# Constant matmuls in front, a fused softmax and merge sums on VectorE, later gate transposes, and the sixth down tile in token halves, in an fp32 encoder block

## The chip, the core and the metric

The kernel runs on one core of one Trainium2 chip. The metric is the device time of one execution in microseconds (us). The kernel before took 915.12 us, the median of 3 runs (915.03 to 915.34). All lines named L... are lines of the kernel before.

## What is computed

One block of a hybrid encoder on 512 tokens of width 1024, all in float32. A combined projection of the normalised input feeds three mixers (a bidirectional mLSTM, a 2-D neighbourhood attention, a cross-attention into 256 memory tokens). Their outputs are merged by sigmoid gates, projected and added to the input; a convolutional gated FFN of width 2816 and a last RMSNorm follow.

```python
h = rms_norm(x, mix_norm_g)
ml_q, ml_k, ml_v, ml_o, ml_gates, na_qkv, xa_q, merge_pre = split(h @ w_in)
y_ml = mlstm_branch(...)              # conv + silu on q, k; two scans over the tokens
y_na = neighbourhood_attention(...)   # softmax over an 8 x 16 window, with a bias
y_xa = memory_cross_attention(...)
merged = sum over the branches of sigmoid(gate) * (y @ w_br)
x = x + merged @ w_out
x = x + (gelu(dwconv3(a)) * u) @ w_down    # a, u = split(rms_norm(x) @ w_up)
return rms_norm(x, final_norm_g)
```

## The kernel before

**Every fp32 product is three matmuls.** Weights and activations are split into a high and a low part in a shorter format. `mm3` (L198) then adds high x high (L199), high x low (L200) and low x high (L201) into one PSUM bank. Activations lie with channels on the partitions and the 512 tokens along the free axis, so one tile of 128 output channels over 1024 input channels is 8 x 3 matmuls of 128x512. Weights come from HBM in blocks of up to 512 KB, three blocks ahead (`emit_raw`, L140, on SyncE's queue SP). One block ahead they are split, the high part by ScalarE (L181) and the low part by VectorE (L182). Activations are split in the same way by `split_act` (L205, L206).

**The order.** The source is written in the order in which TensorE shall work, and a scheduler of the language then orders each engine's own queue, by priority and by what its model takes to be ready. Each engine works its queue in order, so an instruction that waits holds everything behind it on that engine.

1. *Front* (L224 to L322). SP issues the first tile of x, then all the small vectors (`vec`, 720 bytes in each partition), then the first weight block in three pieces, then more of x. ScalarE loads its function table at its first instruction. `x_part` scales and splits a tile of x and squares it, GpSimd adds the squares (L304). TensorE runs 8 steps over the input channels, in each 4 tiles of the mLSTM's query (12 matmuls). The sums of squares over the partitions (`rstd_cols`, L261) and the row of 1/rms spread over all partitions (`rstd_row`, L273) stand inside the last two of these steps.
2. *mLSTM keys, token-major values, gates.* The 4 key tiles, each with a convolution and silu (`conv`, `silu2`), then blocks with tokens on the partitions.
3. *Projections with generators beside them.* `step(n)` (L803) advances a Python generator (`ml_all`, `xa_all`, `na_all`) by n pieces on average, and each piece issues some instructions of a mixer. Calls of `step` after every projection so weave the mixers between the projections' matmuls. `ml_prep` (L431) is the front of the mLSTM: it turns the gates (PE transposes L464), scans them (four scans on VectorE, L470 to L480), copies the result (ScalarE, L481), and turns it back (PE transposes L492).
4. *Merge* (L874 to L909). For each of three branches: four times two gate tiles (L887, evicted by L889 and L890), then two tiles of the branch's output projection. The product with the gate is on VectorE (L905, L907), and the sum over the branches on GpSimd (L908). In the second of the three branches the neighbourhood attention runs beside it: one piece is `scores` of one index (L649), `values` of the index two before and `transposes` of the index one before. The softmax in `scores` is an addition of the bias (L661), a maximum (L663), two exponentials with sums (L666, ScalarE), a reciprocal (L667) and two multiplications (L669).
5. *Output projection, FFN in two halves* of 11 inner tiles (HF = 11). In the second half, six down tiles are computed with channels on the partitions over all 512 tokens. In `last_tiles` (L950) the last two tiles are computed so for the first 256 tokens only, and with tokens on the partitions for the other 256 (two tiles t = 2, 3), so that their norm is a sum along the free axis.
6. *End.* The first 256 tokens are normalised through `cols_a`, `row_a`, `scale_a` and stored as `outa` in two stores of 512 KB. These stand inside and behind tile t = 2, scaled partly on GpSimd. The other 256 tokens are stored as `outb` in four stores of 256 KB; the last two of them end the program.

Of the kernel before, what the change touches and what calls it, by code (L numbers as in the profile page):

```python
# [11 lines left out]
F32 = mybir.dt.float32  # L12
# [15 lines left out]
NU = 15  # L28
RM, RB = 0.75, 1.4
# [71 lines left out]
def hybrid_block(ctx, tc, xT, memT, wflat, vecs, gbias, nabias, outa, outb):  # L101
# [38 lines left out]
    def emit_raw(i):  # L140
        key, n = BLOCKS[i]
        _, off, _ = BINDEX[key]
        r = wp.tile([P, BW], F32, tag="raw", name=nm("wr"), bufs=3)
        src = wflat[off:off + P * n].rearrange("(p n) -> p n", p=P)
        if i == 0:
            for a, b in ((0, P), (P, n // 2), (n // 2, n)):
                SY.dma_start(r[:, a:b], src[:, a:b])
        else:
            SY.dma_start(r[:, :n], src)
        raws[i] = r  # L150

# [15 lines left out]
    def emit_split(i):  # L167
        key, n = BLOCKS[i]
        r = raws.pop(i)
        c, hs = halves(i)  # L170
        split[i] = []
        for a, b in hs:
            m = (b - a) * c
            if key[0] == "dnl":
                h, l = lastw(4 * key[1] + a, m)
            else:
                h = wp.tile([P, HWD], F32R, tag="hi", name=nm("wh"), bufs=4)
                l = wp.tile([P, HWD], F32R, tag="lo", name=nm("wl"), bufs=4)
            for u, v in ((0, P), (P, m)) if i == 0 and a == 0 else ((0, m),):
                src = r[:, a * c + u:a * c + v]  # L180
                A.activation(h[:, u:v], src, AF.Copy)  # L181
                V.tensor_tensor(l[:, u:v], src, h[:, u:v].bitcast(F32), op=ALU.subtract)  # L182
# [40 lines left out]

    load_x(0)  # L224
    SY.dma_start(vec, vecs)
# [71 lines left out]
    def x_part(k):  # L297
        split_act(XH[k], XL[k], xk[k], vcol("mix_g", k))
        if k == 0:
            A.activation(acc, xk[k], AF.Square)  # L300
# [4 lines left out]
        load_x(k + 4)  # L305
# [3 lines left out]
    for k in range(KT):  # L309
# [5 lines left out]
        if k == KT - 2:  # L315
            rc = rstd_cols(acc, S, "x")
        wh, wl = ws[k % 2]
        for f in range(4):
            fs = slice(f * P, (f + 1) * P)
            mm3(ps_q[f], wh[:, fs], wl[:, fs], XH[k], XL[k], k == 0, k == KT - 1)  # L320
            if k == KT - 1 and f == 0:
                rb = rstd_row(rc, S, "x")  # L322
# [22 lines left out]
    def proj(key, XHs, XLs, n=S):  # L345
        ws = weights(key)
        ps = mmps()
        for k in range(KT):
            mm3(ps[:, :n], ws[k][0], ws[k][1], XHs[k], XLs[k], k == 0, k == KT - 1)
        return ps  # L350

# [4 lines left out]
    for f in range(4):  # L356
        ps = proj(("mlk", f), XH, XL)
# [73 lines left out]
    def ml_prep():  # L431
# [40 lines left out]
        on = scr()  # L472
# [4 lines left out]
        cu = scr()  # L477
# [6 lines left out]
        rd = dp.tile([2, 4, S], F32, name="rd")  # L484
        V.tensor_tensor(rr[:36], cu[:36], mr[:36], op=ALU.subtract)
# [22 lines left out]
        yield  # L508
# [110 lines left out]
    def na_all(nq, nk, yh, yl):  # L619
# [29 lines left out]
        def scores(i, ops, bt):  # L649
# [11 lines left out]
            V.tensor_tensor(sm, ps, bt, op=ALU.add)  # L661
            smv = sm.rearrange("p (a b) -> p a b", a=2)
            V.tensor_reduce(mx, smv, axis=AX.X, op=ALU.max, negate=True)  # L663
# [4 lines left out]
            for j in range(2):  # L668
                V.tensor_scalar(smv[:, j, :], smv[:, j, :], su[:, j:j + 1], None, op0=ALU.mult)  # L669
# [204 lines left out]
    for br in range(3):  # L874
# [8 lines left out]
        for fp in range(4):  # L883
            tg = []
            for i in range(2):
                f = 2 * fp + i
                ps = proj(("g", br, f), XH, XL)  # L887
# [4 lines left out]
                step(RATE[br])  # L892
# [5 lines left out]
            for i in range(2):  # L898
# [7 lines left out]
                else:  # L906
                    V.scalar_tensor_tensor(tg[i], tg[i], 1.0, ps, op0=ALU.add, op1=ALU.mult)  # L907
                    G.tensor_tensor(mgv(f), mgv(f), tg[i], op=ALU.add)  # L908
# [36 lines left out]
    def power(v):  # L945
        col = tiny(v.shape[-1])
        half["p"] = G.tensor_tensor(col, v, nhalf[:, :v.shape[-1]], op=ALU.pow)
        return col

    def last_tiles(U, UL_):  # L950
# [3 lines left out]
        for f in range(LF, KT):  # L954
            ps = mmps()[:, :Hf]
            fs = slice((f - LF) * P, (f - LF + 1) * P)
            for k in range(HF):
                mm3(ps, ws[k][0][:, fs], ws[k][1][:, fs], U[k][:, :Hf], UL_[k][:, :Hf], k == 0, k == HF - 1)
            xf = x2[f][:, :Hf]
# [3 lines left out]
            V.tensor_tensor(acc3[:, :Hf], acc3[:, :Hf], sq, op=ALU.add)  # L963
            A.activation(xf, xf, AF.Copy, scale=vcol("fin_g", f))

# [23 lines left out]

        for t in range(2, NT):  # L990
# [16 lines left out]
            for k in range(HF):  # L1007
# [5 lines left out]
                if not last and k == 5:  # L1013
                    cols_a()
                    for i in range(LF):
                        turn(i)
            v0 = sums()
            if not last:
                row_a()
            else:  # L1020
# [6 lines left out]
            else:  # L1027
                A.activation(sq, r, AF.Square, accum_out=ss)
                scale_a(G, 6)
                scale_a(V, 0, 1)  # L1030
# [3 lines left out]
            if not last:  # L1034
                with tc.issue_after(half["p"].ins):
                    scale_a(G, 7)
                scale_a(V, 2, 3)
                store_a(0)
# [9 lines left out]
            if not last:  # L1048
                scale_a(V, 4, 5)
                store_a(4)  # L1050

    for hh in range(2):
# [33 lines left out]
        for f in range(KT if hh == 0 else LF):  # L1086
# [121 lines left out]
```

## Time and profile before

| | |
|---|---|
| median of 3 runs | 915.12 us |
| the profiled execution: its time | 915.78 us |
| the profiled execution: its span, first to last instruction | 914.0 us |
| TensorE (PE) busy | 899.4 us, 98% of the span |
| VectorE (DVE) busy | 581.9 us, 64% |
| ScalarE (ACT) busy | 436.8 us, 48% |
| GpSimd (POOL) busy | 132.2 us, 14% |
| moved by DMA | 96.52 MB, 106 GB/s on average |
| first matmul starts | 5.75 us |
| last matmul of a product starts | 906.84 us |

Rows of a timeline read: start in us, duration in us, engine, line, operation, tile written <- tiles read, shape, count, and in brackets the idle time before with what ended it. Rows of a group read: busy us, mean ns of one | idle us before, and what ended it. PE is the matmul, PEld the weight load that runs beside it. Matmuls are pipelined, and consecutive ones overlap in the rows. Their pace is therefore the distance from one start to the next, and a pause of TensorE can be hidden in a busy share.

### The profile page before, as it was taken

Reading aid. Unit: us, or ns where it says so; the run is one execution under the profiler, and the core shown is the slowest. Engines: PE = TensorE matmul, PEld = TensorE weight load, DVE = VectorE, ACT = ScalarE, POOL = GpSimd, SP = SyncE. Lnnn points to the kernel's source line nnn. Section 1 sums busy time; section 2 is a strip of 40 time slices with the busy share of each in tenths; the row PEclk is TensorE's granted clock in tenths of the full one; section 3 lists DMA queues with packets and bytes.
Section 4 is the critical chain, followed back from the end, with each engine's and each line's share of the span. In section 5 each row is a group of like instructions: output and inputs, shape, how many; then the busy total and the mean of one; then the engine's idle time right before and its main releaser. Section 6 shows DMA issues by size and latency. Waiting matters only on the chain.

```text
span 914.0 us, 12141 instructions
## 1 busy us (share of the span) xinstructions
PE 899.4 (98%) x4456; PEld 752.1 (82%) x4456; DVE 581.9 (64%) x1004; ACT 436.8 (48%) x882; POOL 132.2 (14%) x156
## 2 busy tenths in 40 slices
PE   7999999999999999999999999999999999999997
PEld 5899878988888888788888888888888888888887
DVE  7893666746566668895445547777733477777423
ACT  7464446656545556564333435544422344444432
POOL 5000421102040300111121211111100011111012
PEclk9999999999999999999999999999999999999999
DMA  7233532522242423231223432322233322322412
GB/s 263 96 93 105 175 115 93 161 93 93 70 138 70 134 84 119 91 126 62 92 93 126 137 116 74 112 93 92 87 95 95 114 94 93 93 92 87 132 36 93
DMA packets 32939, 96.52 MB, mean 106 GB/s; under 512 B 4056, under 2 KB 7400, under 8 KB 32880
## 3 DMA queue, kind: packets, MB, share of 16 engines
q1 hardware_dynamic: 31296, 92.31, 31.4%
q0 software_dynamic: 1440, 3.17, 1.4%
q8 instruction: 35, 0.57, 0.3%
q10 hardware_dynamic: 144, 0.26, 0.1%
q14 instruction: 24, 0.20, 0.1%
HBM read 92.57 MB, written 3.16 MB: 105 GB/s over the span
## 4 chain that ended last, share of the span: by engine, by line
PE 95%; DVE 2%; issue 1%; DMA 0%; ACT 0%; POOL 0%; SPq 0%; POOLq 0%; DVEq 0%; ACTq 0%
PE mm L199 28%; PE mm L200 28%; PE mm L201 28%; PE at L552 2%; PE at L199 2%; PE at L200 2%; PE at L201 2%; PE at L688 1%; PE at L675 1%; DMA wr<-wflat 0%; PE at L765 0%; PE at L659 0%; PE at L660 0%; DVE s L907 0%; DVE y L663 0%
## 5 line engine op out<-in xcount | busy, mean ns | idle before, releaser
L199 PE MATMUL mm<-u,wh 128*128 128x512 f32 (+1 forms) x1082 | 425.3, 393 | 5.7 <-ACT wh L181 5.7
L201 PE MATMUL mm<-u,wl 128*128 128x512 f32 (+1 forms) x1082 | 423.1, 391 | 0.0
L200 PE MATMUL mm<-u,wh 128*128 128x512 f32 (+1 forms) x1082 | 422.7, 391 | 0.0
L181 ACT ACTIVATE wh<-wr 128x512 fp32r<-128x512 f32 (+3 forms) x299 | 186.0, 623 | 286.1 <-PE mm L200 244.2
L182 DVE TENSOR_TENSOR wl<-wr,wh 128x512 fp32r<-128x512 f32 (+3 forms) x299 | 232.8, 780 | 126.4 <-ACT wh L181 122.4
L199 PEld LDWEIGHTS mm<-u,wh 128*128 128x128 f32 x1082 | 203.9, 188 | 50.3 <-ACT wh L181 6.2
L201 PEld LDWEIGHTS mm<-u,wl 128*128 128x128 f32 x1082 | 203.7, 188 | 45.7
L200 PEld LDWEIGHTS mm<-u,wh 128*128 128x128 f32 x1082 | 204.0, 189 | 44.2 <-DVE u L206 0.3
L1081 POOL TENSOR_TENSOR s<-s,rb 128x512 f32<-128x512 f32 x22 | 29.1, 1325 | 266.4 <-DVE s L1080 258.3
L908 POOL TENSOR_TENSOR u<-u,s 128x512 f32<-128x512 f32 x16 | 22.4, 1401 | 166.1 <-DVE s L907 108.9
L205 ACT ACTIVATE u<-s 128x512 fp32r<-128x512 f32 x34 | 21.4, 629 | 52.3 <-DVE s L1084 50.6
L889 DVE TENSOR_TENSOR s<-mm,rb_x 128x512 f32<-128x512 f32 x24 | 16.6, 692 | 28.8 <-PE mm L201 28.8
L206 DVE SCALAR_TENSOR_TENSOR u<-s,u 128x512 fp32r<-128x512 f32 x34 | 23.5, 692 | 14.7 <-ACT u L205 14.4
L540 ACT ACTIVATE E<-R,bi 128x128 f32<-128x128 f32 x80 | 27.7, 394 | 4.9 <-POOL R L521 4.6
L334 ACT ACTIVATE s<-pad,vec 128x512 f32<-128x512 f32 x30 | 24.4, 813 | 8.4 <-DVE pad L332 8.4
L335 DVE SCALAR_TENSOR_TENSOR s<-pad,vec,s 128x512 f32<-128x512 f32 x30 | 22.5, 750 | 6.1 <-ACT s L334 6.1
L199 PE MATMUL mm<-wh,u 128*128 128x256 f32 (+1 forms) x80 | 24.5, 306 | 0.0
L200 PE MATMUL mm<-wl,u 128*128 128x256 f32 (+1 forms) x80 | 24.3, 304 | 0.0
L201 PE MATMUL mm<-wh,u 128*128 128x256 f32 (+1 forms) x80 | 24.3, 304 | 0.0
L1091 DVE TENSOR_TENSOR u<-mm,u 128x512 f32<-128x512 f32 x14 | 9.7, 692 | 22.2 <-PE mm L201 22.2
L1080 DVE SCALAR_TENSOR_TENSOR s<-s,s 128x512 f32<-128x512 f32 x22 | 15.2, 692 | 13.4 <-ACT s L1079 13.3
L336 DVE SCALAR_TENSOR_TENSOR s<-pad,vec,s 128x512 f32<-128x512 f32 x30 | 22.5, 750 | 0.7
(250 smaller groups left out, 980.6 us busy)
## 6 DMA issues: line engine op xcount, KB each, us to landing
wr<-wflat SPq DMA_DIRECT2D x141, 512.0 KB, 3.5
s<-xT SPq DMA_DIRECT2D x16, 256.0 KB, 4.3
nab<-nabias SPq DMA_DIRECT2D x16, 256.0 KB, 2.7
wr<-wflat SPq DMA_DIRECT2D x15, 192.0 KB, 2.4
R<-rd SPq DMA_DIRECT2D x8, 256.0 KB, 3.6
u<-nav_d POOLq DMA_DIRECT2D x32, 64.0 KB, 3.0
wr<-wflat SPq DMA_DIRECT2D x2, 544.0 KB, 3.2
s<-memT SPq DMA_DIRECT2D x4, 256.0 KB, 3.7
```

The lines of the kernel that those rows point to most:

```text
L181: A.activation(h[:, u:v], src, AF.Copy)
L182: V.tensor_tensor(l[:, u:v], src, h[:, u:v].bitcast(F32), op=ALU.subtract)
L199: PE.matmul(ps, lh, rh, start=start, stop=False)
L200: PE.matmul(ps, lh, rl, start=False, stop=False)
L201: PE.matmul(ps, ll, rh, start=False, stop=stop)
L206: V.scalar_tensor_tensor(l, src, scale, h.bitcast(F32), op0=ALU.mult, op1=ALU.subtract)
L334: A.activation(t1, pad[:, 0:512], AF.Identity, scale=vcol(w, i), bias=vcol(b, i))
L335: V.scalar_tensor_tensor(t1, pad[:, 1:513], vcol(w, n + i), t1, op0=ALU.mult, op1=ALU.add)
L336: V.scalar_tensor_tensor(t1, pad[:, 2:514], vcol(w, 2 * n + i), t1, op0=ALU.mult, op1=ALU.add)
L540: A.activation(E[:, i, :], src, AF.Exp, bias=bi[:, d, abs(J - s), s, h:h + 1])
L908: G.tensor_tensor(mgv(f), mgv(f), tg[i], op=ALU.add)
L1081: G.tensor_tensor(c, c, rb2, op=ALU.mult)
```

## The change

The edits, in the order of the program; the arithmetic of the block stays the same.

- **Front.** VectorE fills a tile of 128x256 with ones, ScalarE takes one small Tanh of it, and TensorE multiplies it with itself 13 times (128x256 each) into a bank that nobody reads. The first 8 columns of `vec` (the input norm's gains) become a DMA of their own on ScalarE's queue, the rest of `vec` and the gate bias `gb` go to the end of SP's first issues, `gb` no longer on GpSimd's queue. The first and the second weight block are issued in pieces between the tiles of x. The high part of the first 128 weight columns is copied by VectorE instead of ScalarE. The square of tile k of x is issued one step later.
- **Norm of x.** `rstd_cols` and `rstd_row` move from the last two steps of the query into the first key tile (behind its steps 1 and 7), and the first two key tiles use the PSUM banks of the pool `at`.
- **mLSTM gates.** Two scan tiles come from another buffer pool, and one yield of `ml_prep` moves ahead of the subtraction L485, one is dropped at the end, so that the turn back L492 comes one piece later.
- **Softmax.** Addition and maximum are one VectorE instruction per half (tensor_tensor_reduce, x2 per piece), followed by a sign change of the [128, 2] maximum; the two multiplications become one tensor_tensor with a broadcast operand.
- **Merge.** Sums on VectorE instead of GpSimd; half of the `step` of a gate tile is called in the middle of its projection.
- **End.** The sixth tile of the second half (index 5) is computed in two token halves in `last_tiles`. The norm of the first 256 tokens is worked out during its second half, all scaling is on VectorE and both `outa` stores come ahead of t = 2. The column sum for v0 (L1002) moves from behind the tile to behind step 3.

```diff
-        if i == 0:
-            for a, b in ((0, P), (P, n // 2), (n // 2, n)):
-                SY.dma_start(r[:, a:b], src[:, a:b])
-        else:
-            SY.dma_start(r[:, :n], src)
         raws[i] = r
+        if i < 2:
+            cuts = (0, P, n // 2, n) if i == 0 else (0, n // 2, n)
+            return [(r[:, a:b], src[:, a:b]) for a, b in zip(cuts, cuts[1:])]
+        SY.dma_start(r[:, :n], src)
...
-                A.activation(h[:, u:v], src, AF.Copy)
+                if i == 0 and a == u == 0:
+                    V.tensor_copy(h[:, u:v], src)
+                else:
+                    A.activation(h[:, u:v], src, AF.Copy)
...
+    warm = cp.tile([P, 256], F32R, name="warm")
+    V.memset(warm.bitcast(F32), 1.0)
+    A.activation(cp.tile([P, 2], F32, name="first"), warm[:, :2].bitcast(F32), AF.Tanh)
+    pw = atps()
+    for _ in range(WARM):
+        PE.matmul(pw[:, :256], warm[:, :P], warm, start=True, stop=True)
+    A.dma_start(vec[:, :8], vecs[:, :8])
+    w0, w1 = emit_raw(0), emit_raw(1)
+    st["raw"] = 2
     load_x(0)
-    SY.dma_start(vec, vecs)
-    emit_raw(0)
-    for k in range(1, 4):
-        load_x(k)
-    emit_raw(1)
-    st["raw"] = 2
-    G.dma_start(gb, gbias[0:16].partition_broadcast(P))
+    SY.dma_start(*w0[0])
+    SY.dma_start(*w0[1])
+    load_x(1)
+    SY.dma_start(*w0[2])
+    load_x(2)
+    SY.dma_start(*w1[0])
+    load_x(3)
+    SY.dma_start(*w1[1])
+    SY.dma_start(vec[:, 8:], vecs[:, 8:])
+    SY.dma_start(gb, gbias[0:16].partition_broadcast(P))
...
+    def proj(key, XHs, XLs, n=S, bank=None, at={}):
+        ws = weights(key)
+        ps = (bank or mmps)()
+        for k in range(KT):
+            mm3(ps[:, :n], ws[k][0], ws[k][1], XHs[k], XLs[k], k == 0, k == KT - 1)
+            if k in at:
+                at[k]()
+        return ps
...
+    ps_k = [proj(("mlk", 0), XH, XL, bank=atps, at={1: lambda: norm.append(rstd_cols(acc, S, "x")),
+                                                    7: lambda: norm.append(rstd_row(norm[0], S, "x"))})]
+    rc, rb = norm
+    ps_k.append(proj(("mlk", 1), XH, XL, bank=atps))
...
-            V.tensor_tensor(sm, ps, bt, op=ALU.add)
             smv = sm.rearrange("p (a b) -> p a b", a=2)
-            V.tensor_reduce(mx, smv, axis=AX.X, op=ALU.max, negate=True)
+            for j in range(2):
+                js = slice(j * M, (j + 1) * M)
+                V.tensor_tensor_reduce(smv[:, j, :], ps[:, js], bt[:, js], 1.0, 2.0 * NEG, ALU.add, ALU.max,
+                                       accum_out=mx[:, j:j + 1])
+            V.tensor_scalar(mx, mx, -1.0, None, op0=ALU.mult)
...
-            for j in range(2):
-                V.tensor_scalar(smv[:, j, :], smv[:, j, :], su[:, j:j + 1], None, op0=ALU.mult)
+            V.tensor_tensor(smv, smv, su.unsqueeze(2).to_broadcast([P, 2, M]), op=ALU.mult)
...
-                ps = proj(("g", br, f), XH, XL)
+                ps = proj(("g", br, f), XH, XL, at={3: lambda: step(RATE[br] / 2)})
...
-                step(RATE[br])
+                step(RATE[br] / 2)
...
-                    G.tensor_tensor(mgv(f), mgv(f), tg[i], op=ALU.add)
+                    V.tensor_tensor(mgv(f), mgv(f), tg[i], op=ALU.add)
...
+        for f in range(LF - 1, KT):
+            half_tile(f, slice(0, Hf))
...
+        half_tile(LF - 1, slice(Hf, S), {5: cols_a, HF - 1: row_a})
+        for i in (0, 4):
+            scale_a(V, *range(i, i + 4))
+            store_a(i)
...
+                if k == 3:
+                    v0 = sums()
...
-        for f in range(KT if hh == 0 else LF):
+        for f in range(KT if hh == 0 else LF - 1):
```

Here `half_tile(f, cs, at)` is the old loop body of `last_tiles` for the token range `cs`; it calls `at[k]()` behind step k and takes the weights of tile 5 from its own two blocks.

More of the change, by code (lines that the diff above doesn't have):

```diff
@@ L471, in ml_prep @@
         V.tensor_tensor_scan(mr[32:36, ::-1], lr[32:36, ::-1], pl[96:100, ::-1], NEG, op0=ALU.add, op1=ALU.max)
-        on = scr()
+        on = tp.tile([P, 2 * M], F32, tag="nab", name=nm("on"))
         G.memset(on[:36], 1.0)
@@ L476, in ml_prep @@
         G.memset(onv[32:36, :, P - 1:P], 0.0)
-        cu = scr()
+        cu = tp.tile([P, 2 * M], F32, tag="nab", name=nm("cu"))
         G.memset(cu[:36], 0.0)
@@ L1012, in last_tiles @@
                     A.activation(r, pts[1][:, 256:], AF.Copy)
-                if not last and k == 5:
-                    cols_a()
+                if k == 3:
+                    v0 = sums()
+                if not last and k == HF - 3:
                     for i in range(LF):
                         turn(i)
[L1017 to L1020, printed above, removed]
+            if last:
                 for i in range(LF):
@@ L1033, in last_tiles @@
             col = power(v)
[L1034 to L1038, printed above, removed]
             oa, ob = scr(), scr()
```

44 lines of the change are left out of this document (20 added, 24 removed).

## The prediction

> **What bounds the kernel now.** I read the page first, then the waits of TensorE, then the timeline of the stretches which those waits name.
>
> The page:
>
> ```profile
> span 914.0 us, 12141 instructions
> ...
> PE 899.4 (98%) x4456; PEld 752.1 (82%) x4456; DVE 581.9 (64%) x1004; ACT 436.8 (48%) x882; POOL 132.2 (14%) x156
> ```
>
> TensorE is busy for 98% of the span and the change takes no product away from it. So the most that can be won is what TensorE does not spend on products at full pace: 914.0 - 899.4 = 14.6 us of idleness, and whatever part of its busy time runs slowly. Its waits, all of them (us in total, times, longest):
>
> ```profile
> PE mm L199 <- ACT wh L181: 5.7, 1, 5.7
> PE at L688 <- DVE s L680: 1.2, 1, 1.2
> PE at L492 <- ACT s L481: 0.7, 1, 0.7
> PE at L675 <- DVE s L669: 0.6, 1, 0.6
> PE at L688 <- ACT s L678: 0.2, 1, 0.2
> ```
>
> Five waits, 8.4 us: one of 5.7 us before the first matmul, one of 0.7 us at the turned-back gates, and three of together 2.0 us in the neighbourhood attention. The other 6 us lie behind the last product. The front, queue by queue (SP, ScalarE, VectorE, then TensorE around 11 us):
>
> ```profile
> 0.74 0.38 SPq L221 DMA_DIRECT2D s<-xT  x1
> 1.17 0.42 SPq L225 DMA_DIRECT2D vec<-vecs  x1
> 1.64 1.37 SPq L147 DMA_DIRECT2D wr<-wflat  x3
> ```
>
> ```profile
> 0.73 1.28 ACT L300 ACT_TABLE_LOAD   x1 [0.73 <-PEq L1199]
> 3.82 0.63 ACT L300 ACTIVATE acc_x<-s 128x512 f32<-128x512 f32 x1 [1.81 <-DMA s<-xT]
> 4.36 0.70 ACT L205 ACTIVATE u<-s,vec 128x512 fp32r<-128x512 f32 x1
> 5.38 0.31 ACT L181 ACTIVATE wh<-wr 128x128 fp32r<-128x128 f32 x1 [0.32 <-DMA wr<-wflat]
> 6.52 0.52 ACT L181 ACTIVATE wh<-wr 128x384 fp32r<-128x384 f32 x1 [0.83 <-DMA wr<-wflat]
> ```
>
> ```profile
> 5.10 0.75 DVE L206 SCALAR_TENSOR_TENSOR u<-s,vec,u 128x512 fp32r<-128x512 f32 x1 [0.81 <-ACT u L205]
> 5.77 0.29 DVE L182 TENSOR_TENSOR wl<-wr,wh 128x128 fp32r<-128x128 f32 x1
> 7.08 0.56 DVE L182 TENSOR_TENSOR wl<-wr,wh 128x384 fp32r<-128x384 f32 x1 [1.02 <-ACT wh L181]
> ```
>
> ```profile
> 10.68 0.63 PE L201 MATMUL mm<-u,wl 128*128 128x512 f32 x1
> 11.10 0.55 PE L199 MATMUL mm<-u,wh 128*128 128x512 f32 x1
> 11.49 0.39 PE L200 MATMUL mm<-u,wh 128*128 128x512 f32 x1
> 11.72 0.39 PE L201 MATMUL mm<-u,wl 128*128 128x512 f32 x1
> ```
>
> ```profile
> 8.00:10.00 2.00, 2.00 (x6) 1.52 (x6) 1.93 (x3) 2.00 (x4) 0.18 (x1) 1.00 0.91 358
> ```
>
> The first weight piece (the first of the three at 1.64) lands at 5.38; its high part takes 0.31 us, and the first matmul starts at 5.75. From start to start, a 512-wide matmul takes 0.42 us until 11.10 and 0.23 us from 11.49 on. So for 5.35 us (5.75 to 11.10) TensorE ran the 12 matmuls of the first step at about half pace, though the clock column of the windows (the 1.00 ahead of the last two numbers) shows nothing of it. That is busy time in the page, and yet some 2.4 us lost.
>
> **The change, part by part.**
>
> *Front, start.* The first weight piece takes `vec`'s place in SP's queue, 1.17 instead of 1.64, and lands 0.47 us earlier, near 4.9. VectorE copies it in about the 0.29 us of the row of that size: first matmul at 5.2. The other operand needs x (landed at 3.82), the 8 gains and ScalarE's 0.70 us. The gains' DMA is issued near 0.73 if it goes ahead of the table load, and behind table load and Tanh near 2.2. Its landing time is not in the trace; the larger transfer took
>
> ```profile
> vec<-vecs SPq DMA_DIRECT2D x1, 90.0 KB, 2.8
> ```
>
> so the operand is ready near 4.6, or near 5.7. A landing as slow as the first weight piece's (1.64 to 5.38) on top would make 6.6. I take 5.2 for the first matmul, with 6.6 as the end below nothing. The square leaves ScalarE ahead of the scaling, which only helps.
>
> *Front, pace.* 13 matmuls of 256 columns at half of 0.42 us are 2.7 us. VectorE's fill, for which no row stands, is between the 0.29 us of a 128-wide operation here and the 0.75 us of a 512-wide one; with 0.35 us the burst runs from about 1.1 to 3.8, in time in which TensorE waits for DMA. It costs nothing as long as the first operands land later than that. What it gains is the unknown. The trace shows one fact: 5.35 us after TensorE's first matmul the pace doubles. I take it that this counts from the first constant matmul and that a pause of some 1.4 us does not undo it; then the fast pace comes at about 6.5. By then the front waits for data anyway. The second weight piece lands at 6.52 - 0.47 = 6.05, its high part is ready at 6.6 and its low part, with 0.56 us, at 7.15. From there 7 matmuls are left in the step, 7 x 0.23 = 1.6: the second step begins at 8.8 instead of 11.10. With the thirteenth matmul, which still took 0.39, the front gains 2.4 us. If the pace doubles only 5.35 us after 5.2, the gain is 0.55; if data keeps up with the fast pace from 5.2 on, the step ends at 8.0 and the gain is 3.3.
>
> [...]
>
> *Norm of x.* The same matmuls in another place: 0 on TensorE. The query's convolutions start later, and the first two keys hold two banks until VectorE reads them. The bank of the second key must be free when the fourth token tile of the next stage starts, a whole key tile and more behind; 0.
>
> *Gate transposes.* The wait of 0.7 us at L492 is for the four scans and the copy behind them. A whole projection comes between after the change. What is late next, the turned-back rows, is needed two pieces later. 0.7 us gained, between 0 and 0.8.
>
> *Attention.* The wait of 1.2 us is for L680. VectorE right in front of it, and POOL's row of that time:
>
> ```profile
> 372.06 1.41 DVE L182 TENSOR_TENSOR wl<-wr,wh 128x512 fp32r<-128x512 f32 x1
> 373.39 0.67 DVE L663 TENSOR_REDUCE y<-s 128x2 f32<-128x512 f32 x1
> ```
>
> ```profile
> 371.61 1.30 POOL L908 TENSOR_TENSOR u<-u,s 128x512 f32<-128x512 f32 x1 [1.69 <-DVE s L907]
> ```
>
> ```profile
> 353.00:375.00 22.00, 20.74 (x125) 17.62 (x124) 20.14 (x35) 14.93 (x34) 2.59 (x2) 1.00 0.32 99
> ```
>
> VectorE is busy for 20.14 of 22 us here, it is the limit of this stretch. And a weight split takes 1.41 us while GpSimd sums. The groups of VectorE in the attention (busy us, mean ns):
>
> ```profile
> L182 DVE TENSOR_TENSOR wl<-wr,wh 128x512 fp32r<-128x512 f32 x26 | 19.6, 754 | 7.6 <-ACT wh L181 7.6
> L669 DVE TENSOR_SCALAR s<-s,y 128x256 f32<-128x256 f32 x32 | 13.0, 447 | 0.3
> L661 DVE TENSOR_TENSOR s<-at,nab 128x512 f32<-128x512 f32 x16 | 10.9, 680 | 0.0
> L663 DVE TENSOR_REDUCE y<-s 128x2 f32<-128x512 f32 x16 | 10.8, 676 | 0.1
> ```
>
> A sum moved to VectorE costs about the 0.68 us of L661. What it removes is a collision, 1.41 - 0.68 = 0.73 us each: about even in VectorE's time, better where the collision lies ahead of an instruction that TensorE awaits. The fused operation has one relative in the trace, from SBUF alone and as wide:
>
> ```profile
> 907.69 0.43 DVE L1026 CUSTOM_DVE_ANT_0 s<-s 128x256 f32<-128x256 f32 x1
> 908.04 0.08 DVE L1026 DVE_READ_ACCUMULATOR2_ANT y<- 128x1 f32 x1
> ```
>
> Per piece 2 x (0.43 + 0.08) + about 0.2 for the sign = 1.2 us replace 0.68 + 0.68 = 1.36. One broadcast multiplication at 0.68 replaces two of L669 at 0.45 = 0.9. So a piece gives back some 0.4 us, and right in front of L680 at least one collision (the row at 372.06) and one piece lie: about 1.1 us against a wait of 1.2. The half steps in the middle of a gate tile also bring fewer pieces back to back. I take all three waits as gone, 2.0 us, between 0 (the waits only move) and 3.0 (with the restart of the pipeline behind each).
>
> *End.* Tile 5 in halves is the same columns in twice the matmuls: 0 within 0.1. L1002 comes ahead of the last product:
>
> ```profile
> 906.96 0.28 PE L1002 MATMUL at<-ones,acc 128*128 128x1 f32 x2
> ```
>
> 0.2 us lost. The last stores have the queue to themselves, since both `outa` stores are issued earlier. Before, one was 2.3 us ahead of the last:
>
> ```profile
> 907.68 0.52 SPq L988 DMA_DIRECT2D outa<-u  x1
> 909.95 0.33 SPq L1047 DMA_DIRECT2D outb<-s  x1
> ```
>
> ```profile
> outb<-s SPq DMA_DIRECT2D x3, 256.0 KB, 2.9
> outb<-s ACTq DMA_DIRECT2D x1, 256.0 KB, 2.4
> ```
>
> A store takes 2.4 to 2.9 us to land, so between 0 and 0.5 us is gained; I take 0.2. The end gives 0, between -0.5 and +0.5.
>
> **Sum:** 2.4 + 0.7 + 2.0 + 0 = 5.1 us. The profiled execution took 915.78, its span 914.0, so 1.78 us lie around the span and stay. It would take 910.7. It stood 0.66 above the median of the runs; on the median, 915.12 - 5.1 = 910.0.
>
> **Rivals.**
>
> *The burst does not count.* The pace doubles 5.35 us after the first real matmul, or the change doesn't do what it says, since the scheduler sets the burst late, or the gains' DMA. For it: the burst of 2.7 us is shorter than the 5.35 us and a pause follows it. Against it: nothing in the trace says that the pause resets. Front 0.55 instead of 2.4: 911.9. [...]
>
> *The attention's waits stay.* Behind each merge group `step` still asks for 1.6 pieces at once, and the sums now stand in VectorE's own queue between L907 and the softmax. For it: VectorE at 20.14 of 22 us. Against it: the collision right in front of the longest wait. 915.12 - 3.1 = 912.0. With the first rival together: 913.9.
>
> *VectorE becomes the bound, and the kernel slower.* The mechanism is a fused operation that runs slower from PSUM than L1026 from SBUF. A merge group of the attention has 3 x 1.6 = 4.8 pieces, 9.6 fused operations. VectorE has 22 - 20.14 = 1.9 us to spare in the tight group. Four groups must lose 3.1 + 1.8 = 4.9 us before the kernel is slower by 0.2%, 1.2 each, so VectorE's work must grow by 3.1 per group: from 4.8 x 1.36 = 6.5 to 9.6, that is 1.0 us for each fused operation, twice the 0.51 of the row. At 1.3 us it would be 12.5 - 6.5 - 1.9 = 4.1 per group and 915.1 - 3.1 + 16.4 = 928.4. Against it: the row, and L661, which reads PSUM at 0.68 for twice the width.
>
> **How the numbers follow.** The forecast has 0.56, the burst that doesn't count 0.20, the waits that stay 0.15, both 0.05, slower 0.04. About 0.2% (1.8 us) is what a measurement can tell from no change. The first three lie more than that below 915.12, but for 0.01 at their edge: faster 0.90. Both rivals together are the same, with that edge: 0.06. Slower 0.04. The forecast with all its bounds good (3.3 + 0.8 + 3.0 + 0.5 = 7.6) would be 907.5; I cut there at 907.8, and reach above to 912.9, past the two single rivals at 911.9 and 912.0.
>
> **What would show it.** In the profile after: first real matmul near 5.2 and steps of 0.23 us within it from 6.5 on; no wait at L492's successor; the attention's waits for VectorE under 0.5 us in all, and no weight split above 0.8 us there; fused operations at 0.5 us or less; the last two stores landing 2.4 us after their issue. I am wrong in the front if steps of 0.42 us last past 9, in the attention if TensorE's waits for VectorE keep their sum.

## The result and the profile after

The changed kernel takes 910.88 us (median of 6 runs, 909.93 to 911.15) against 915.22 us for the kernel before (6 runs, 915.03 to 915.65): 4.34 us less, ratio 0.995 with the interval 0.9937 to 0.9963. The forecast was 910.0. The profiled execution is the fastest of the six, 909.93 us with a span of 908.1; beside before's profiled 915.78 that is 5.85 us. So one sum has to explain 5.9 us in a pair of traces and 4.3 us in the medians, and that gap was the first thing to find out.

The page of the changed kernel, and its waits of TensorE (us in total, times, longest). From here on, L... in a row is a line of the kernel that the row comes from:

```profile
span 908.1 us, 12239 instructions
...
PE 900.4 (99%) x4502; PEld 755.2 (83%) x4502; DVE 579.5 (64%) x1059; ACT 436.8 (48%) x884; POOL 107.5 (12%) x136
```

```profile
PE at L233 <- DVE warm L229: 1.2, 1, 1.2
PE mm L202 <- ACT u L208: 0.3, 1, 0.3
PE mm L203 <- DVE u L209: 0.3, 1, 0.3
PE at L705 <- DVE s L699: 0.2, 1, 0.2
```

The waits at the gates and in the attention are gone but for 0.2 us; TensorE now begins at 1.2 us, with the constant matmuls. Its front:

```profile
1.19 3.14 PE L233 MATMUL at<-warm 128*128 128x256 f32 x13 [1.19 <-DVE warm L229]
4.66 0.49 PE L202 MATMUL mm<-u,wh 128*128 128x512 f32 x1 [0.34 <-ACT u L208]
...
5.79 0.39 PE L204 MATMUL mm<-u,wl 128*128 128x512 f32 x1
6.02 0.40 PE L202 MATMUL mm<-u,wh 128*128 128x512 f32 x1
```

The first real matmul starts at 4.66 (before: 5.75), and from 5.79 on one follows each 0.23 us. VectorE's groups in the attention (busy us, mean ns):

```profile
L185 DVE TENSOR_TENSOR wl<-wr,wh 128x512 fp32r<-128x512 f32 x28 | 19.2, 687 | 9.9 <-ACT wh L184 8.2 <-PE at L688 1.5
L692 DVE CUSTOM_DVE_ANT_0 s<-at,nab 128x256 f32<-128x256 f32 x32 | 12.5, 418 | 0.0
...
L692 DVE DVE_READ_ACCUMULATOR2_ANT y<- 128x1 f32 x32 | 2.7, 83 | 0.0
```

The fused operation costs 418 + 83 ns, as L1026 of before suggested, and the weight split is back at 687 ns from 754.

To see where the time came from, follow the same VectorE instruction through both programs: an eviction waits for its product, so its start marks TensorE's progress. Four such marks and the last sum, of before and then of after:

```profile
111.75 0.69 DVE L821 TENSOR_TENSOR u<-mm,rb_x 128x512 f32<-128x512 f32 x1 [1.64 <-PE mm L201]
152.63 0.69 DVE L830 TENSOR_TENSOR s<-mm,rb_x 128x512 f32<-128x512 f32 x1 [1.59 <-PE mm L201]
337.88 0.69 DVE L889 TENSOR_TENSOR s<-mm,rb_x 128x512 f32<-128x512 f32 x1 [1.59 <-PE mm L201]
448.15 0.69 DVE L889 TENSOR_TENSOR s<-mm,rb_x 128x512 f32<-128x512 f32 x1 [0.47 <-PE mm L201]
907.25 0.41 DVE L1023 TENSOR_TENSOR s<-mm,s 128x256 f32<-128x256 f32 x1
```

```profile
109.30 0.69 DVE L851 TENSOR_TENSOR u<-mm,rb_x 128x512 f32<-128x512 f32 x1 [1.64 <-PE mm L204]
149.38 0.69 DVE L860 TENSOR_TENSOR s<-mm,rb_x 128x512 f32<-128x512 f32 x1 [1.59 <-PE mm L204]
334.64 0.69 DVE L919 TENSOR_TENSOR s<-mm,rb_x 128x512 f32<-128x512 f32 x1 [1.59 <-PE mm L204]
442.31 0.69 DVE L919 TENSOR_TENSOR s<-mm,rb_x 128x512 f32<-128x512 f32 x1 [1.35 <-PE mm L204]
901.97 0.42 DVE L1063 TENSOR_TENSOR s<-mm,s 128x256 f32<-128x256 f32 x1 [1.92 <-PE mm L204]
```

The first row of each gives the front: 111.75 - 109.30 = 2.45 us gained. From there the distances between marks tell each stage by itself: to the second mark (the gates) 40.88 and 40.08, gained 0.80; from the third to the fourth (the attention) 110.27 and 107.67, gained 2.60; from the fourth to the last sum 459.10 and 459.66, lost 0.56; from it to the span's end (913.96 and 908.13, unrounded) 6.72 and 6.16, gained 0.56. Together 5.85. The same marks in one profiled execution of each later kernel, the distances from unrounded times. Where the pace doubles is an estimate from the distances between the matmuls' starts, good to some 0.2 us:

| kernel | first real matmul | pace doubles | front mark | gates | attention | to the last sum | tail | span |
|---|---|---|---|---|---|---|---|---|
| before | 5.75 | 11.1 to 11.5 | 111.75 | 40.88 | 110.27 | 459.10 | 6.72 | 914.0 |
| after | 4.66 | by 4.7 | 109.30 | 40.07 | 107.67 | 459.65 | 6.16 | 908.1 |
| again | 4.57 | 10.8 | 111.01 | 40.07 | 107.69 | 459.64 | 6.17 | 909.8 |
| warm0 | 4.62 | 8.3 | 109.89 | 40.07 | 107.70 | 459.64 | 6.15 | 908.7 |
| warm16 | 4.77 | by 5.5 | 109.91 | 40.07 | 107.73 | 459.64 | 6.16 | 908.8 |
| warm22 | 6.05 | 7.2 | 109.58 | 40.07 | 107.71 | 459.65 | 6.16 | 908.4 |
| warm28 | 6.58 | by 6.6 | 109.58 | 40.07 | 107.72 | 459.59 | 6.26 | 908.3 |
| u_yield | 4.50 | 9.0 | 110.08 | **40.87** | 107.64 | 460.00 | 6.18 | 910.0 |
| u_merge | 4.48 | 9.3 | 110.53 | 40.07 | **109.41** | 459.55 | 6.44 | 911.3 |
| u_soft | 4.58 | 10.8 | 110.98 | 40.07 | 107.70 | 459.66 | 6.16 | 909.9 |
| u_half | 4.56 | by 4.6 | 109.11 | 40.07 | 107.90 | 459.58 | 6.41 | 908.3 |
| u_end | 4.59 | 10.8 | 111.01 | 40.07 | 107.67 | **459.24** | **7.34** | 910.6 |
| u_vec | **5.00** | 13.1 | 112.81 | 40.07 | 107.69 | 459.65 | 6.25 | 911.7 |
| b_merge | 6.05 | 10.5 | 111.43 | 40.88 | **107.75** | 459.23 | 6.73 | 911.2 |

A stage whose code is the same repeats from execution to execution: the gates to 0.01 us, the attention of the unaltered code between 107.64 and 107.73, the way to the last sum within 0.1 but for u_yield's 460.00, which nothing here explains, the tail within 0.3. The front mark alone wanders widely, from 109.11 to 111.01 in executions with one and the same front. So the edits are read from single traces by stage, and the front from many runs.

### The profile page after: what moved, and what is told of

It reads as the page before. It is cut to its first block, busy times and chain, and to the rows that moved or that the text cites. A ratio compares the mean times of both kernels' runs of the same rounds, so it can differ in the third digit from the quotient of the medians.

```text
span 908.1 us, 12239 instructions
## 1 busy us (share of the span) xinstructions
PE 900.4 (99%) x4502; PEld 755.2 (83%) x4502; DVE 579.5 (64%) x1059; ACT 436.8 (48%) x884; POOL 107.5 (12%) x136
## 4 chain that ended last, share of the span: by engine, by line
PE 96%; DVE 1%; issue 1%; ACT 1%; DMA 1%; SPq 0%; POOLq 0%; POOL 0%; DVEq 0%
PE mm L202 28%; PE mm L203 28%; PE mm L204 28%; PE at L202 2%; PE at L203 2%; PE at L204 2%; PE at L580 2%; PE at L718 1%; PE at L705 1%; DMA s<-xT 1%; PE at L795 0%; PE at L688 0%; PE at L687 0%; PE at L283 0%; PE at L604 0%
## 5 line engine op out<-in xcount | busy, mean ns | idle before, releaser
L202 PE MATMUL mm<-u,wh 128*128 128x512 f32 (+1 forms) x1077 | 420.6, 391 | 0.5 <-ACT u L208 0.3
L203 PE MATMUL mm<-u,wh 128*128 128x512 f32 (+1 forms) x1077 | 417.4, 388 | 0.3 <-DVE u L209 0.3
L204 PE MATMUL mm<-u,wl 128*128 128x512 f32 (+1 forms) x1077 | 417.2, 387 | 0.0
L184 ACT ACTIVATE wh<-wr 128x512 fp32r<-128x512 f32 (+1 forms) x298 | 185.6, 624 | 285.6 <-PE mm L203 241.5
L185 DVE TENSOR_TENSOR wl<-wr,wh 128x512 fp32r<-128x512 f32 (+3 forms) x299 | 228.7, 766 | 121.4 <-ACT wh L184 114.9
L208 ACT ACTIVATE u<-s 128x512 fp32r<-128x512 f32 x34 | 21.4, 630 | 53.1 <-DVE s L1114 50.6
L964 POOL TENSOR_TENSOR acc<-acc,s 128x512 f32<-128x512 f32 x7 | 9.1, 1298 | 223.1 <-ACT s L963 223.1
L367 DVE TENSOR_TENSOR pad<-mm,rb 128x512 f32<-128x512 f32 x22 | 15.1, 692 | 11.6 <-PE mm L204 11.6
```

The costliest lines, as they stand in the source:

```text
L202: PE.matmul(ps, lh, rh, start=start, stop=False)
L203: PE.matmul(ps, lh, rl, start=False, stop=False)
L204: PE.matmul(ps, ll, rh, start=False, stop=stop)
L208: A.activation(h, src, AF.Copy, scale=scale)
```

## The experiments

**The constant matmuls.** The kernel once more, and other counts:

```diff
-WARM = 13
+WARM = 0
```

That is warm0; warm16, warm22 and warm28 have their number there, and again is unaltered.

> The changed kernel once more, unaltered. Its six runs so far lie between 909.93 and 911.15 us, and the one execution with a profile, in which TensorE ran at the fast pace (0.23 us a step) from its first real matmul at 4.66 us on, was the fastest of them. Theory A (the moment at which the pace doubles is not tied to the kernel's own start; where it falls in the front differs from execution to execution): the runs spread again over about 1 us, and this profile may show the doubling at another place, anywhere from 4.7 to about 9 us, with a span longer by half of the time that was spent at the slow pace. Theory B (the pace doubles a fixed time after the first constant matmul; the spread has another place): the fast pace holds from the first real matmul again, and a span longer than 908.1 us differs from the first profile behind the front.

> The changed kernel without the 13 constant matmuls (the count set to 0), all else as it is. Both theories: the first real matmul stays near 4.7 us and its step runs at 0.42 us a matmul. Theory B: the pace doubles 5.35 us behind it as before, at 10.0 us, step 2 begins near 9.8 instead of 8.39, so 1.4 us slower than the first profiled execution: 911.3 us, and the spread of the runs stays as it is. Theory A: it doubles at a moment that differs between executions, 8 to 11.5 us; step 2 begins between 9.5 and 9.8 in all of them, so the runs lie closer together than those with the burst, at 911.3 to 911.8 us. If the burst does nothing at all: the same time as the changed kernel, 910.9 us.

> The changed kernel with 16 constant matmuls instead of 13: they end near 5.0 us instead of 4.33 and close the pause of 0.34 us ahead of the first real matmul, which starts up to 0.4 us later. [...] Theory B: the fast pace from the first real matmul at about 5.0 us, step 2 waits for data as it did: 910.0 to 910.5 us, with a spread that has nothing to do with the front. If it is the pause that sometimes sets the pace back: the spread goes, and the median falls to about 910.0 us.

> The changed kernel with 28 constant matmuls: at 0.21 us each they reach to 7.2 us, less where the pace doubles within them (opened at 4.6 us they would end at 5.9). Theory A: the real matmuls run at the fast pace from their first one in nearly every execution; it starts between 5.9 and 7.2, step 2 begins between 8.6 and 10.0, so the runs lie between 910.1 and 911.6 us, the median near the changed kernel's own, 910.9, or up to 0.5 above. Theory B: the constant matmuls themselves run at 0.11 us each from about 4.6 us on, the first real one starts at 5.9, step 2 at 8.6: 910.1 us in the front's account, in every execution alike.

> The changed kernel with 22 constant matmuls, which reach to 5.9 us at the slow pace. With 13 the pace doubled at 4.7 to 10.9 us in six profiled executions, with 16 at 5, with 28 near 6. [...] If the length alone counts and 22 is too short: the median is that of 13, 910.9 to 911.0 us.

TensorE's front in the second execution of the unaltered kernel:

```profile
1.19 3.15 PE L233 MATMUL at<-warm 128*128 128x256 f32 x13 [1.19 <-DVE warm L229]
4.57 0.80 PE L202 MATMUL mm<-u,wh 128*128 128x512 f32 x1 [0.23 <-ACT u L208]
...
10.22 0.63 PE L202 MATMUL mm<-u,wh 128*128 128x512 f32 x1
10.64 0.46 PE L203 MATMUL mm<-u,wh 128*128 128x512 f32 x1
10.94 0.39 PE L204 MATMUL mm<-u,wl 128*128 128x512 f32 x1
```

The same burst at the same moment, and the slow pace (0.43 us a matmul) until 10.64, 6.07 us behind the first real matmul. This execution is 1.71 us behind the first one at the front mark (111.01 against 109.30), and 1.71 behind at the last sum (903.68 against 901.97). What the rows show to differ between the two is where the pace doubled. In seven profiled executions with this burst it doubled by 4.6 and by 4.7, at 9.0 and 9.3, and three times at 10.8. (By 4.6 is u_half: the rows at 5.69, 5.92 and 6.15 are 0.23 us apart already.) Nor is it a fixed time after the first real matmul: some 6.2 us in this execution, 3.7 in warm0, 5.7 in the kernel before and 4.5 in b_merge, which has the front of the kernel before.

The runs say the same: again 911.03 us (910.00 to 911.62, 5 runs) and warm0 910.99 (910.48 to 911.60, 5 runs). In the median the 13 constant matmuls are worth nothing. A few more are worth something: warm16 910.33 (909.98 to 910.55), warm28 910.16 (909.38 to 910.47), warm22 910.01 (909.59 to 910.25), 5 runs each; against before in the same batches warm22's ratio is 0.9939 (0.9926 to 0.9951), again's 0.995 (0.9937 to 0.9962). The intervals overlap, the runs hardly do: all 15 runs of the three are at or below 910.55; of the 11 with 13 constant matmuls, 8 are above it. The front of warm22:

```profile
1.19 5.07 PE L233 MATMUL at<-warm 128*128 128x256 f32 x22 [1.19 <-DVE warm L229]
6.05 0.63 PE L202 MATMUL mm<-u,wh 128*128 128x512 f32 x1
...
6.90 0.54 PE L204 MATMUL mm<-u,wl 128*128 128x512 f32 x1
7.28 0.39 PE L202 MATMUL mm<-u,wh 128*128 128x512 f32 x1
```

The first real matmul has no idle time in front of it, here and in warm16 and warm28, where the 13 left 0.16 to 0.34 us; the fast pace is there by 5.5 (16), 7.2 (22) and 6.6 (28). Theory B (a fixed time after the first constant matmul) met the times of 16 and 28, and has fallen all the same: the same burst at the same moment was followed by the fast pace by 4.7 and at 10.8. Of theory A the main part stands, a moment that isn't tied to the kernel's start; its forecast that 28 would have a median of 910.9 or more missed. The sentence about the pause came nearest: where the burst reaches the first product, the late cases are gone. Whether it is the pause or the length isn't shown, since 16 are also longer than 13; and the pause's length doesn't sort the seven executions, for the two early ones had 0.34 and 0.24 us and the one with 0.16 doubled at 9.3. Without a pause the pace doubled within some 6.0 us of the start at 1.19 in each of the three traces. Behind a burst of 3.15 us and a pause the fast pace came at once in two executions of seven, and no run here shows what made the difference.

**The first loads.** The gains in their old place:

```diff
-    A.dma_start(vec[:, :8], vecs[:, :8])
     load_x(0)
+    SY.dma_start(vec, vecs)
     SY.dma_start(*w0[0])
...
-    SY.dma_start(vec[:, 8:], vecs[:, 8:])
```

> The changed kernel with the vector of gains loaded whole in its old place, in SP's queue ahead of the first weight piece, instead of 8 of its columns by ScalarE's queue and the rest last. If the early start (first real matmul at 4.6 instead of 5.75 us) comes from the 90 KB that went ahead of the first weight piece: the piece lands about 1 us later and the first real matmul is back at 5.4 to 5.8 us, and later by that much everything behind it, apart from the moment at which the pace doubles. If it comes from VectorE's copy in ScalarE's place, or from the table load that stands earlier: it stays at 4.6 to 4.9 us.

913.21 us (9 runs, 912.31 to 913.55), 2.3 us above the changed kernel. Its longest wait:

```profile
PE mm L202 <- ACT wh L184: 1.5, 1, 1.5
```

The first real matmul, at 5.00, missed the 5.4 to 5.8: the first weight piece lands only 0.45 us later (its copy at 4.51 instead of 4.06), and what the matmul waits for is the scaled x:

```profile
3.70 0.63 ACT L323 ACTIVATE acc_x<-s 128x512 f32<-128x512 f32 x1 [1.48 <-DMA s<-xT]
4.24 0.70 ACT L208 ACTIVATE u<-s,vec 128x512 fp32r<-128x512 f32 x1
```

The gains are there by 3.92, when VectorE first reads them; the scaling (L208) stands behind the square (L323) here, where the changed kernel starts it at 3.89. What the 90 KB delay is the second weight piece, whose high part starts at 6.71 instead of 5.04, and TensorE stands for 1.5 us behind its first matmul. That is a pause too, and the pace doubles at 13.1. The front mark lies at 112.81, 1.8 us behind the changed kernel's late executions (111.0) and even behind the kernel before (111.75) in these traces: what stays gained in the front hangs on the gains being out of the weights' way. The expectation had the wrong piece.

**The gate transposes.**

```diff
         rd = dp.tile([2, 4, S], F32, name="rd")
-        yield
         V.tensor_tensor(rr[:36], cu[:36], mr[:36], op=ALU.subtract)
...
         ml.update(rd=rd, em=em, bi=bi)
+        yield
```

> The changed kernel with the two yields of ml_prep put back where they were (the transposes of the turned-back gates again one projection earlier), all else as it is. My account: the wait of 0.7 us for the copy behind the scans comes back in the profile and from there to the end every eviction is 0.6 to 0.8 us later against those ahead of it; it is seen in the trace, since the moment at which the pace doubles moves the whole execution by up to 1.7 us. The rival account, that the earlier start of everything (2.4 us in the front) or the scans' other buffers took the wait away: no wait comes back, 0.0 us.

The wait is back,

```profile
PE at L520 <- ACT s L509: 0.7, 1, 0.7
```

and the gates' stage takes 40.87 us instead of 40.07: 0.80, all of it this edit's. (911.41 us, 4 runs, 910.89 to 912.01.)

**The attention: three edits undone one by one, and one done alone.**

```diff
-                    V.tensor_tensor(mgv(f), mgv(f), tg[i], op=ALU.add)
+                    G.tensor_tensor(mgv(f), mgv(f), tg[i], op=ALU.add)
```

That is u_merge; b_merge is the kernel before with the same line changed the other way, and nothing else. u_soft:

```diff
-                V.tensor_tensor_reduce(smv[:, j, :], ps[:, js], bt[:, js], 1.0, 2.0 * NEG, ALU.add, ALU.max,
-                                       accum_out=mx[:, j:j + 1])
-            V.tensor_scalar(mx, mx, -1.0, None, op0=ALU.mult)
+            V.tensor_tensor(sm, ps, bt, op=ALU.add)
+            V.tensor_reduce(mx, smv, axis=AX.X, op=ALU.max, negate=True)
...
-            V.tensor_tensor(smv, smv, su.unsqueeze(2).to_broadcast([P, 2, M]), op=ALU.mult)
+            for j in range(2):
+                V.tensor_scalar(smv[:, j, :], smv[:, j, :], su[:, j:j + 1], None, op0=ALU.mult)
```

u_half:

```diff
-                ps = proj(("g", br, f), XH, XL, at={3: lambda: step(RATE[br] / 2)})
+                ps = proj(("g", br, f), XH, XL)
...
-                step(RATE[br] / 2)
+                step(RATE[br])
```

> The changed kernel with the merge sums back on GpSimd, all else as it is. If the collision is what the waits came from: weight splits on VectorE take up to 1.4 us again while GpSimd sums, and at least the wait of 1.2 us in the second merge group comes back: 0.8 to 1.5 us between the first and the last merge group. If the sums are even in VectorE's time and the softmax or the half steps made the room (VectorE at 18.9 of 22 us in the tight stretch, 3.1 us free): the collisions are seen on VectorE, but TensorE's waits stay under 0.4 us and the stretch keeps its length within 0.2 us.

> The changed kernel with the old softmax (sum, reduction, two multiplications) instead of the fused operation and the one multiplication, all else as it is. A piece then costs VectorE 0.68 + 0.68 + 2 x 0.45 = 2.26 instead of 2 x (0.42 + 0.08) + 0.16 + 0.69 = 1.85 us: 0.4 us each, 1.9 a merge group, and the tight stretch goes from 18.9 to about 20.8 of 22 us. If VectorE's total is what the waits came from: 0.8 to 1.5 us come back between the first and the last merge group. If collisions or the bunching of pieces were the cause: under 0.4 us.

> The changed kernel with one whole step behind each gate tile instead of two half ones, all else as it is. If the bunching of pieces made the waits: a wait of about 1 us comes back in the attention, with VectorE's busy time in its stretches as it is now. If VectorE's total or the collisions made them: within 0.3 us of the changed kernel between the first and the last merge group.

> The kernel before with one edit: the merge sums of the last two branches on VectorE instead of GpSimd. Putting them back on GpSimd in the changed kernel cost 1.7 us in the attention, undoing the softmax or the half steps under 0.2. If the collisions with GpSimd are the whole cause: the waits of 1.2 and 0.6 us for VectorE go, no weight split stands above 0.8 us there, and 2.0 to 2.5 us are gained between the first and the last merge group: 912.8 to 913.3 us. If VectorE's total is the limit (it has 20.1 of 22 us in the tight stretch, and the sums add some 0.7 us each less the collisions they end): the waits stay or grow, 0 to 0.7 us gained. As in my own account, the sums about even and the rest from the softmax: near 0.7 us.

Without the softmax's edit the attention takes 107.70 us, without the half steps 107.90, against 107.67 to 107.73 with both: 0.0 and 0.2 us (911.01 us and 910.76 us, 4 runs each). With the sums on GpSimd it takes 109.41, 1.74 us more than in the changed kernel and past the 0.8 to 1.5 expected, and the kernel 912.80 us (6 runs, 911.71 to 913.14). That is still 0.86 us less than the 110.27 of the kernel before: so the softmax and the half steps, the other edits of this stage, seem to be worth that much where GpSimd sums, and nothing once it doesn't. No run tried them alone in the kernel before. The waits of u_merge, then VectorE and GpSimd in front of the longer one:

```profile
PE at L718 <- DVE s L710: 1.1, 1, 1.1
PE at L705 <- DVE s L699: 0.6, 1, 0.6
```

```profile
367.01 1.77 DVE L185 TENSOR_TENSOR wl<-wr,wh 128x512 fp32r<-128x512 f32 x1 [0.16 <-ACT wh L184]
...
369.99 1.31 DVE L185 TENSOR_TENSOR wl<-wr,wh 128x512 fp32r<-128x512 f32 x1
371.22 0.15 DVE L694 TENSOR_SCALAR y<-y 128x2 f32<-128x2 f32 x1
371.29 0.68 DVE L710 COPY s<-at 128x512 f32<-128x512 f32 x1
```

```profile
366.93 1.30 POOL L938 TENSOR_TENSOR u<-u,s 128x512 f32<-128x512 f32 x1 [22.62 <-DVE s L937]
369.46 1.29 POOL L938 TENSOR_TENSOR u<-u,s 128x512 f32<-128x512 f32 x1 [1.23 <-DVE s L937]
```

Two weight splits fall beside GpSimd's sums and take 1.77 and 1.31 us instead of 0.69; L710, which TensorE waits for, stands behind them. VectorE's total doesn't decide here. Over the four stretches from 331 to 415 us the sums of the windows of u_merge and of the changed kernel are:

```profile
sum 84.00, PE 82.29 PEld 70.63 DVE 66.30 ACT 51.32 POOL 7.74; mean PE 20.57 PEld 17.66 DVE 16.57 ACT 12.83 POOL 1.94
```

```profile
sum 84.00, PE 83.83 PEld 72.08 DVE 67.42 ACT 52.97 POOL 0.00; mean PE 20.96 PEld 18.02 DVE 16.86 ACT 13.24 POOL 0.00
```

For each us of TensorE's work VectorE is busy for 66.30 / 82.29 = 0.81 us in the one and 67.42 / 83.83 = 0.80 in the other: what the sums cost VectorE, the collisions cost it too. TensorE lost 1.5 us more in the first, because of where the collisions stood. u_soft's VectorE is busy for 72.70 us in these windows, more than the 70.59 of the kernel before, and TensorE waits for it for 0.2 us in the whole attention.

And the sums alone, put into the kernel before, bring nearly the whole of it: b_merge's attention takes 107.75 us instead of 110.27, 2.52 of the 2.60 us and about the top of the 2.0 to 2.5 expected, and the kernel 913.51 us (10 runs, 912.96 to 914.39), a little above the 912.8 to 913.3, ratio 0.9979 (0.997 to 0.9988). Its waits and its groups show how:

```profile
PE mm L199 <- ACT wh L181: 6.1, 1, 6.1
PE at L492 <- ACT s L481: 0.7, 1, 0.7
PE at L688 <- ACT s L678: 0.2, 1, 0.2
```

```profile
L182 DVE TENSOR_TENSOR wl<-wr,wh 128x512 fp32r<-128x512 f32 x26 | 17.8, 684 | 6.6 <-ACT wh L181 6.4
...
L669 DVE TENSOR_SCALAR s<-s,y 128x256 f32<-128x256 f32 x32 | 9.8, 346 | 0.1
```

Both waits for VectorE are gone. And L669, 447 ns in the kernel before, takes 346 ns where GpSimd is still. The 447 were not a price that each one paid: three of the 32 took 1.39 to 1.42 us, each beside a sum, the other 29 0.35.

**The end as it was.** The edit puts the old `last_tiles` back, with the sixth down tile whole:

```diff
-        for f in range(KT if hh == 0 else LF - 1):
+        for f in range(KT if hh == 0 else LF):
```

> The changed kernel with the end as it was (the sixth down tile whole, the first half's sums, row and stores inside the third token tile), all else as it is. My account: the end is worth 0, between -0.5 and +0.5 us, read as the distance from the last full evictions ahead of the down tiles to the span's end. The trace of the changed kernel has the last two stores in an empty queue and a span that ends 5.6 us behind the last product instead of 6.0: by that reading 0.2 to 0.6 us are lost again, with both the outa stores and the outb stores in the queue between 906 and 912 us.

912.26 us (5 runs, 912.00 to 912.61), above the changed kernel's 910.88. The last sum comes 0.41 us sooner (459.24 instead of 459.65), the tail is 7.34 instead of 6.16 us: 0.8 us lost in all, above the 0.2 to 0.6 expected. The last store on ScalarE's queue (us from issue to landing) of u_end, then of the changed kernel:

```profile
outb<-s ACTq DMA_DIRECT2D x1, 256.0 KB, 3.3
```

```profile
outb<-s ACTq DMA_DIRECT2D x1, 256.0 KB, 2.0
```

In the changed kernel the last big store was issued 8.3 us ahead of it, in u_end 2.0. That nearness alone doesn't give the 3.3: in the kernel before and in b_merge the big store was issued 2.1 us ahead, and the same store took 2.4, with a tail of 6.72 and 6.73. Why the old end does worse behind the new stages is open.

## Why the prediction was right, and where it was not

The sum of 5.1 us stands between the 5.9 us of the profiled pair and the 4.3 us of the medians. Four of its steps did not go as they were told, and their errors cancel in part: in the typical execution the front gave 0.74 instead of 2.4 us, the attention 2.60 instead of 2.0. That 910.0 came within 0.9 us of the median is partly luck.

*Front, pace: failed in the typical execution.* "I take it that this counts from the first constant matmul and that a pause of some 1.4 us does not undo it" is the step. The profiled execution has the forecast's 2.4 (2.45), though by an earlier start and an earlier fast pace than told (4.66 and 4.7 instead of 5.2 and 6.5). The pause was 0.16 to 0.34 us instead of 1.4 and the fast pace still came at 9.0 to 10.8 in five executions of seven; and the 5.35 us that the step counts with is one execution's figure; others have some 3.7 to 6.2. By the prediction's own sign, "I am wrong in the front if steps of 0.42 us last past 9", the front is wrong in those at 9.3 and 10.8. In the median the first rival happened: with and without the burst 911.03 and 910.99 us. (Its own figure of 911.9 was too high, since the other stages gave more.) What stays of the front in the late executions is 111.75 - 111.01 = 0.74 us, from one execution of each kernel; b_merge, with the front of before, has its mark at 111.43. The other stages give 0.80 + 2.60 - 0.56 + 0.56 = 3.4, and with 0.74 that is 4.1, near the median's 4.3.

*Front, start: mis-sized.* 4.5 to 4.7 instead of 5.2. The first weight piece landed 2.9 us behind its issue (1.18 to 4.06), where I had carried over 3.7 us from the kernel before. The piece took 2.9 also behind the gains in u_vec, so it isn't the gains that slowed it before; that the other pieces and x are issued in another order in the changed kernel and in u_vec is a difference left, not tried by itself.

*Norm of x: 0 forecast, not measured by itself.* Its share lies within the front's distance, and no run puts it back.

*Gate transposes: right.* 0.7 forecast, 0.80 measured, by the edit alone.

*Attention: right in sign, 2.0 forecast and 2.60 measured, with the shares put wrong.* The sentence on the sums (about even in VectorE's time, better where the collision lies ahead of an instruction that TensorE awaits) is what happened, and it is nearly the whole: 2.52 us alone. The step that failed is "One broadcast multiplication at 0.68 replaces two of L669 at 0.45". The 0.45 was itself a price with collisions in it; without GpSimd it is 0.346, two of them 0.69, and the broadcast multiplication (0.689) saves nothing. I had seen the collision in the weight split and taken the mean of the neighbouring row as undisturbed. The half steps, told of as bringing fewer pieces back to back, brought 0.2 at most beside the other edits. Nor was VectorE, at 20.14 of 22 us, "the limit of this stretch": the same row has TensorE at 20.74, and u_soft gives VectorE more to do than the kernel before without its waits.

*End: 0 forecast, 0.56 - 0.56 = 0 measured, by luck.* Of the 0.56 lost ahead of the last sum, 0.41 belong to the end's edit (u_end), more than the 0.2 told, and 0.13 came with the sums (459.23 in b_merge), which no wait explains. The tail gave 0.56, more than the 0.2; the store that ends the program landed 2.5 us after its issue instead of 2.9.

*The other rivals.* The attention's waits did not stay, and VectorE did not become the bound: the fused operation took 0.50 us, half of the 1.0 from which it would have cost time.

A version better than both kernels came out of this: the changed kernel with 22 constant matmuls, 910.01 us, its highest run (910.25) below 9 of the 11 of the changed kernel. The two were not run side by side; the kernel before had medians of 915.22 to 915.53 beside them.

## What to carry to other kernels

Let a constant burst ahead of the first product reach up to it without a pause: here only the bursts that did were worth something in the median (910.01 to 910.33 us, against 911.03 with 13 and 910.99 with none). Price it over many runs, since one trace shows only one place of the doubling. Before pricing an operation by the mean of its group, look whether another engine was at work beside it: a mean with collisions in it (L669: 447 ns, 346 without the sums beside it) made the cure look like a saving of two things. And an engine's busy total didn't tell here whether it holds up TensorE (VectorE was busy for 66.30 us in the four stretches of u_merge and for 67.42 in the changed kernel, and TensorE lost 1.5 us more in the first): look at what stands in front of the instruction that is awaited.

## What the runs showed of the hardware

- Two executions of one kernel differed by 1.71 us from the front mark to the last sum, with the moment at which TensorE's pace doubled (by 4.7 and at 10.8 us) as the difference that shows.
- Beside a 512-wide sum on GpSimd (1.29 us) a 512-wide two-input operation on VectorE took 1.06 to 1.41 us in the kernel before and 1.30 to 1.82 in four rows of u_merge, instead of 0.69. The fused operation, which reads one input from PSUM, was not slowed by the sums: in u_merge the four at 342.87, 343.21, 369.30 and 369.64 lay beside one and took 0.41 us each, and all 32 average 416 ns (418 in the changed kernel). This one lies within the sum at 369.46:

```profile
369.64 0.41 DVE L692 CUSTOM_DVE_ANT_0 s<-at,nab 128x256 f32<-128x256 f32 x1
```
